# Differential attention mixer of a two-layer encoder: shorter vector work, some weight splitting on GpSimd, another order of steps

## The chip, the cores and the metric

The kernel runs on one core of a Trainium2 chip. The metric is the device time of one execution in microseconds, as the median of three runs. The engines are called PE (matmuls, with PEld for its weight loads), DVE (vector), ACT (scalar), POOL or GpSimd, and SP (which only issues DMAs here).

## What is computed

A trunk of two layers over 256 tokens of width 1024. Each layer is a half-step SwiGLU block (inner width 2816), a token mixer and a second half-step SwiGLU block, each behind an RMS norm. Layer 0 mixes with gated linear attention (GLA), layer 1 with differential attention, which the change is about:

```python
def diff_mixer(h, w_in, qk_norm_g, lam_vecs, subln_g, w_out, rel_table, lam_init):
    q, k, v = jnp.split(h @ w_in, [DIFF_QK, 2 * DIFF_QK], axis=-1)
    q = rms_norm(q.reshape(B, S, DIFF_HEADS, 2, DIFF_DH), qk_norm_g[0]) * (DIFF_DH ** -0.5)
    k = rms_norm(k.reshape(B, S, DIFF_HEADS, 2, DIFF_DH), qk_norm_g[1])
    ...
        p1 = jax.nn.softmax(jnp.einsum('bhqd,bhkd->bhqk', q1b, k1) + bias, axis=-1)
        p2 = jax.nn.softmax(jnp.einsum('bhqd,bhkd->bhqk', q2b, k2) + bias, axis=-1)
        return jnp.einsum('bhqk,bhkv->bhqv', p1 - lam * p2, vh)
    ...
    out = rms_norm(out, subln_g) * (1.0 - lam_init)
    return out.reshape(B, S, DIFF_V) @ w_out
```

There are 8 heads of 2 x 64 channels for q and k and 128 for v. All is float32.

## The kernel before

**Weights.** PE multiplies in a reduced form of float32 (`FR`), so each weight and each activation is held as a high part and a low part and each product is three matmuls. `weight_plan` (L61) lists all weight pieces in the order of use, numbered w0, w1 and so on. `prefetch` issues their DMAs on SP into three stage buffers; `parts` (L156) splits a staged piece in two halves of 128 x 1024 elements: ACT writes the high part (a copy, L192 in the profile, since both are issued from one helper line), DVE the low part, whole minus high (also L192). The results lie in five buffers `w`. A stage buffer is free again when its last low part is written. v's weights are pieces 125 and 126 (heads 0 to 3, in two halves of the inner dimension), 129 (heads 4 and 5) and 130 (heads 6 and 7); 131 to 134 belong to the output projection.

**The mixer** (`diff`, from L848). PE works on the projection in small pieces: a piece is 12 matmuls of 512 columns for q, k and the first v group, or 24 of 256 columns for the others. Heads go in four pairs. The steps of pair n are

- `b` qk_stats: from the sums of squares (L882 on ACT, L883 on DVE) the inverse square root of q's and k's mean squares, `dr`, and the scaled q and k, `qkx` (L900);
- `n` qk_norm: PE transposes them (L908), ACT and DVE write the high and low part (`qkn`);
- `s` softmax of one head: scores (L925), DVE adds the bias and takes the row maximum (L932), negates the maxima (L936), ACT takes the exponential and its sums (L940), DVE scales and subtracts the second map (L942 to L948);
- `f` flip: PE transposes the maps (L959);
- `a` attend: maps times v (L993), ACT squares (`dosq`, L997), DVE sums and takes the inverse root, `dro`, and writes the scaled output `do` (L1002);
- `o` normalize: PE transposes `do` (L1010), ACT and DVE write its parts for the output projection.

**The order.** The string `ORDER` (L46) lists these steps and pieces (`h`) as the program issues them. PE follows that order to the letter; the other engines run the instructions that the steps give them in an order that a scheduler fixes when the program is built. Every engine runs its own list strictly in sequence. `hold` keeps back weight splitting until the last pair is through. The last flip, attend and normalize stand inside the output projection. An inverse square root is the function `rsqrt` (L259): two integer steps for a first guess, then three Newton rounds of three instructions, 11 in all on DVE. It serves the norms, q and k (`dr`), the attention output (`dro`) and the GLA output.

Of the kernel before, what the change touches and what calls it, by code (L numbers as in the profile page):

```python
# [11 lines left out]
F32 = mybir.dt.float32  # L12
# [31 lines left out]


ORDER = """  # L46
h h h h h h b0 h h h n0 b1 h s00 s01 h n1 h h h f0 h s10 s11 h b2 h n2 a0 h f1 s20 s21 h a1 o0 h b3 h h f2 n3 o1 a2 s30 s31 h h o2 hold
"""


# [9 lines left out]

def weight_plan(w):  # L61

    plan = []

    def cols(a, start, width=CW, times=1, shift=BESIDE_X):
        plan.append((a[:, start : start + width], KD, width, times, shift))

    def wide(a, c, nk=KD, shift=WIDE_X):

        for k0 in range(0, nk, WK):  # L70
            n = min(WK, nk - k0)
            plan.append((a[k0 * P : (k0 + n) * P, c * WW : (c + 1) * WW], n, WW, 1, shift))

    def both(a, b):

        for k0 in range(0, KD, WK):
            plan.append((tuple(z[k0 * P : (k0 + WK) * P, :CW] for z in (a, b)), WK, WW, 1, WIDE_X))

    def ffn(i, j):
        gu, down = w["ffn_w_gu"][i, j], w["ffn_w_down"][i, j]  # L80
        for c in range(FF // CW):
            cols(gu, c * CW)
            cols(gu, FF + c * CW)
        if (i, j) == (1, 1):
            for c in range(D // WW):
                wide(down, c, NFB, WIDE_A)
            return
        for dc in range(D // CW):
            for k0 in range(0, NFB, KD):
                n = min(KD, NFB - k0)  # L90
                plan.append((down[k0 * P : (k0 + n) * P, dc * CW : (dc + 1) * CW], n, CW, 1, BESIDE_A))
# [12 lines left out]
    ffn(0, 1)  # L104
    ffn(1, 0)
    for kind, c in DIFF_COLS.split():
        a, c = w["diff_w_in"][0], int(c)
        if kind == "a":
            both(a[:, c * CW :], a[:, D + c * CW :])
        elif kind == "b":  # L110
            wide(a[:, 2 * D :], c)
        else:
            cols(a, 2 * D + c * CW)
    for c in range(4):
        cols(w["diff_w_out"][0], c * CW, shift=BESIDE_A)
    ffn(1, 1)
    return plan
# [3 lines left out]
def trunk(ctx: ExitStack, tc: tile.TileContext, ins, out):  # L121
# [34 lines left out]
    def parts():  # L156

        i = state["split"]
        _, nk, width, times, shift = plan[i]
        t = staged.pop(i)  # L160
        n = nk * 2 * times * width
        whole = wpool.tile([P, 2 * KD * CW + W_PAD], FR, tag="w", name=f"w{i}")
        w = split[i] = whole[:, shift : shift + n].rearrange("p (k h c) -> p k h c", h=2, c=times * width)
        state["split"] += 1
        step = 2 if i < 2 or width == WW else 4
        for k0 in range(0, nk, step):
            ks = slice(k0, min(k0 + step, nk))
            whole, wh, wl = t[:, ks, :], w[:, ks, 0, :], w[:, ks, 1, :]
            if times > 1:
                shape = [P, whole.shape[1], times, width]  # L170
                whole = whole[:, :, None, :].broadcast_to(shape)
                wh, wl = (z.rearrange("p k (c n) -> p k c n", c=times) for z in (wh, wl))
            high = partial(nc.scalar.activation, wh, whole, AF.Copy)
            low = partial(nc.vector.tensor_tensor, out=wl, in0=whole, in1=wh.bitcast(F32), op=ALU.subtract)
            yield high, low

    def split_weights(n):
# [93 lines left out]

# [576 lines left out]
    def diff(norm, nxt):  # L848
        with ExitStack() as octx:
# [21 lines left out]
            raw, tot, qkx, qkn, bias, sc, v_tm, dT, ov, eps = ({} for _ in range(10))  # L871

            def qk_done(hp):
                def done(t, pq):
                    raw[hp, t] = pq
                    if t == 0:
                        tot[hp] = small.tile([P, 2, 2, 4], F32, tag="dtot", name=f"dtot{hp}")
# [5 lines left out]
                    nc.vector.tensor_reduce(out=tot[hp][:, :, t], in_=sq.rearrange("p (i g d) -> p i g d", i=2, d=64), axis=AX.X, op=ALU.add)  # L883

                return done

            def qk_stats(hp):
# [3 lines left out]
                    src = bass.AP(frel_d.tensor, frel_d.offset + 2 * hp * (2 * T - 1) + P * qt, [[1, P], [2 * T - 1, 2], [1, T]])  # L891
                    nc.sync.dma_start(bias[hp][:, qt], src)

                for t in range(2):
                    nc.vector.tensor_scalar(out=tot[hp][:, :, t, :], in0=tot[hp][:, :, t, :], scalar1=1.0 / 64, scalar2=evx[:, t : t + 1], op0=ALU.mult, op1=ALU.add)
                r = rsqrt(tot[hp].rearrange("p i t g -> p (i t g)"), [P, 16], "dr").rearrange("p (i t g) -> p i t g", i=2, t=2)
                qkx[hp] = d2.tile([P, 2, 2, CW], F32, tag="qkx", name=f"qkx{hp}", bufs=1)
                for t in range(2):
                    v4 = [z.rearrange("p i (g d) -> p i g d", d=64) for z in (qkx[hp][:, :, t], raw.pop((hp, t)).rearrange("p (i c) -> p i c", i=2))]
                    nc.vector.tensor_tensor(out=v4[0], in0=v4[1], in1=r[:, :, t, :, None].broadcast_to([P, 2, 4, 64]), op=ALU.mult)  # L900
# [17 lines left out]
            def softmax(hp, b):  # L918
# [67 lines left out]
            def attend(c):  # L986
# [11 lines left out]
                nc.vector.scalar_tensor_tensor(out=dtot, in0=dtot, scalar=1.0 / P, in1=eps.pop(c), op0=ALU.mult, op1=ALU.add)  # L998
# [94 lines left out]
```

## Time and profile before

| | |
|---|---|
| runs shown | 994.36, 995.04, 996.09 us; median 995.04 |
| profiled execution | 995.94 us, its span in the profile 994.1 |
| busy | PE 983.7, DVE 745.6, ACT 565.3, POOL 1.4 us |
| PE's clock | full in every slice of the span |
| differential mixer | 686.2 to 803.0 us of the span |

The span is what the profile covers of the execution; 1.8 us lie around it. A line such as "PE a L1 <- DVE b L2: 1.8, 2, 0.9" says that PE, before the instruction of line 1 that writes a, waited in two places for DVE's instruction of line 2, 1.8 us in all. Matmuls are pipelined and their ends are modelled.

### The profile page before, as it was taken

Reading aid. Unit: us, or ns where it says so; the run is one execution under the profiler, and the core shown is the slowest. Engines: PE = TensorE matmul, PEld = TensorE weight load, DVE = VectorE, ACT = ScalarE, POOL = GpSimd, SP = SyncE. Lnnn points to the kernel's source line nnn. Section 1 sums busy time; section 2 is a strip of 40 time slices with the busy share of each in tenths; the row PEclk is TensorE's granted clock in tenths of the full one; section 3 lists DMA queues with packets and bytes.
Section 4 is the critical chain, followed back from the end, with each engine's and each line's share of the span. In section 5 each row is a group of like instructions: output and inputs, shape, how many; then the busy total and the mean of one; then the engine's idle time right before and its main releaser. Section 6 shows DMA issues by size and latency. Waiting matters only on the chain.

```text
span 994.1 us, 14886 instructions
## 1 busy us (share of the span) xinstructions
PE 983.7 (99%) x5890; PEld 871.5 (88%) x5890; DVE 745.6 (75%) x1275; ACT 565.3 (57%) x946; POOL 1.4 (0%) x9
## 2 busy tenths in 40 slices
PE   9999999999999999999999999999999999999998
PEld 8788888998889888888888888888788998888887
DVE  6988757499977997875679787556998699877640
ACT  6756545298756765643456555435486567665430
POOL 0000000000000000000000000000000000000000
PEclk9999999999999999999999999999999999999999
DMA  9776554665322775555557555475661258755530
GB/s 307 249 241 197 170 180 123 192 220 183 123 85 85 254 253 178 193 164 185 171 176 247 194 187 174 134 230 174 228 191 66 82 183 260 236 170 177 184 127 22
DMA packets 166787, 178.87 MB, mean 180 GB/s; under 512 B 4579, under 2 KB 155550, under 8 KB 166718
## 3 DMA queue, kind: packets, MB, share of 16 engines
q1 hardware_dynamic: 166318, 177.71, 55.3%
q8 instruction: 46, 0.75, 0.3%
q10 hardware_dynamic: 400, 0.21, 0.1%
q14 instruction: 23, 0.19, 0.1%
HBM read 176.84 MB, written 1.06 MB: 179 GB/s over the span
## 4 chain that ended last, share of the span: by engine, by line
PE 69%; DVE 4%; ACT 2%; issue 1%; DMA 0%; SPq 0%; ACTq 0%
PE ps_u L216 12%; PE ps_g L216 12%; PE ps_d L216 8%; PE ps_g L217 6%; PE ps_u L217 6%; PE ps_d L217 4%; PE ps_d L232 2%; PE ps_d L231 2%; PE ps_d L233 2%; DVE w L192 2%; PE ps_s L681 1%; PE ps_w L209 1%; PE ps_w L210 1%; PE ps_w L211 1%; PE ps_g L231 1%; PE ps_g L233 1%
## 5 line engine op out<-in xcount | busy, mean ns | idle before, releaser
L192 DVE TENSOR_TENSOR w<-stage,w 128x1024 fp32r<-128x1024 f32 x332 | 384.2, 1196 | 32.9 <-ACT w L192 32.7
L192 ACT ACTIVATE w<-stage 128x1024 fp32r<-128x1024 f32 x332 | 326.9, 1036 | 61.6 <-DMA stage<-in_ffn_w_gu_dram 16.1
L216 PE MATMUL ps_g<-x,w 128*128 128x512 f32 x704 | 246.6, 392 | 0.8 <-ACT w L506 0.8
L216 PE MATMUL ps_u<-x,w 128*128 128x512 f32 x704 | 246.3, 392 | 0.0
L217 PE MATMUL ps_u<-x,w 128*128 128x256 f32 x704 | 196.9, 280 | 0.0
L217 PE MATMUL ps_g<-x,w 128*128 128x256 f32 x704 | 196.5, 280 | 0.0
L216 PE MATMUL ps_d<-a,w 128*128 128x512 f32 x528 | 183.2, 390 | 0.0
L216 PEld LDWEIGHTS ps_g<-x,w 128*128 128x128 f32 x704 | 132.0, 188 | 30.5 <-ACT w L506 1.1
L216 PEld LDWEIGHTS ps_u<-x,w 128*128 128x128 f32 x704 | 132.2, 188 | 29.0
L217 PE MATMUL ps_d<-a,w 128*128 128x256 f32 x528 | 148.9, 282 | 0.0
L217 PEld LDWEIGHTS ps_g<-x,w 128*128 128x128 f32 x704 | 132.0, 188 | 0.3
L217 PEld LDWEIGHTS ps_u<-x,w 128*128 128x128 f32 x704 | 132.2, 188 | 0.0
L216 PEld LDWEIGHTS ps_d<-a,w 128*128 128x128 f32 x528 | 99.1, 188 | 20.8
L217 PEld LDWEIGHTS ps_d<-a,w 128*128 128x128 f32 x528 | 99.8, 189 | 0.0
L327 ACT ACTIVATE x<-x,par 128x256 fp32r<-128x256 f32 x40 | 20.0, 507 | 117.3 <-DVE x L380 117.3
L256 ACT COPY half<-ps_u 128x256 f32<-128x256 f32 x88 | 32.5, 370 | 81.8 <-PE ps_u L217 80.9
L256 ACT COPY half<-ps_g 128x256 f32<-128x256 f32 x88 | 32.1, 368 | 73.1 <-PE ps_g L217 72.2
L257 DVE TENSOR_TENSOR gate<-ps_g,half 128x256 f32<-128x256 f32 x88 | 36.6, 420 | 38.6 <-ACT half L256 38.6
L257 DVE TENSOR_TENSOR up<-ps_u,half 128x256 f32<-128x256 f32 x88 | 36.6, 420 | 36.4 <-ACT half L256 36.4
L380 DVE SCALAR_TENSOR_TENSOR x<-ps_d,x 128x256 f32<-128x256 f32 x48 | 20.3, 423 | 57.9 <-PE ps_d L217 56.6
L232 PE MATMUL ps_d<-w,a 128*128 128x512 f32 (+1 forms) x110 | 38.2, 347 | 0.0
L231 PE MATMUL ps_d<-w,a 128*128 128x512 f32 (+1 forms) x110 | 38.2, 347 | 0.0
(241 smaller groups left out, 1344.2 us busy)
## 6 DMA issues: line engine op xcount, KB each, us to landing
stage<-in_ffn_w_gu_dram SPq DMA_DIRECT2D x86, 1024.0 KB, 5.2
stage<-in_ffn_w_down_dram SPq DMA_DIRECT2D x34, 1024.0 KB, 5.3
stage<-in_gla_w_in_dram SPq DMA_DIRECT2D x12, 1024.0 KB, 6.7
stage<-in_ffn_w_down_dram SPq DMA_DIRECT2D x12, 768.0 KB, 4.4
stage<-in_diff_w_in_dram SPq DMA_DIRECT2D x16, 512.0 KB, 5.0
stage<-in_gla_w_out_dram SPq DMA_DIRECT2D x4, 1024.0 KB, 5.5
stage<-in_diff_w_in_dram SPq DMA_DIRECT2D x4, 1024.0 KB
stage<-in_diff_w_out_dram SPq DMA_DIRECT2D x4, 1024.0 KB, 5.7
```

What stands on the lines that cost most here:

```text
L192: op()
L209: mm(ps, lhsT=w[:, k, 0, ms], rhs=act[:, k, 0, :], start=first, stop=False)
L210: mm(ps, lhsT=w[:, k, 0, ms], rhs=act[:, k, 1, :], start=False, stop=False)
L216: mm(ps, lhsT=w[:, wk, 0, ms], rhs=act[:, k, :, :], start=first, stop=False)
L217: mm(ps[:, 0:T], lhsT=w[:, wk, 1, ms], rhs=act[:, k, 0, :], start=False, stop=last)
L231: mm(ps, lhsT=act[:, k, 0, ts_], rhs=w[:, wk, 0, cs], start=k == 0, stop=False)
L232: mm(ps, lhsT=act[:, k, 0, ts_], rhs=w[:, wk, 1, cs], start=False, stop=False)
L233: mm(ps, lhsT=act[:, k, 1, ts_], rhs=w[:, wk, 0, cs], start=False, stop=k == nk - 1)
L256: nc.scalar.copy(h[:, b, :], ps[:, T:512])
L257: nc.vector.tensor_tensor(out=out_t[:, b, :], in0=ps[:, 0:T], in1=h[:, b, :], op=ALU.add)
L327: high = nc.scalar.activation(self.x2[:, d, 0, :], src, AF.Copy, scale=g)
L380: nc.vector.scalar_tensor_tensor(out=x[:, d, :], in0=ps[:, h * T : (h + 1) * T], scalar=coef, in1=x[:, d, :], op0=ALU.mult, op1=ALU.add,)
```

## The change

Five edits:

- `rsqrt` has nine instructions: after the first guess one round of four and one of three.
- The affine step of the q/k statistics and the eps term of the output norm take one instruction for what was two (L895 and L946), with another layout of the sums.
- The scores are negated as the bias is added, so that the row minimum can go to the exponential as it is; the negation L936 is gone, and an exponential reads only its own minimum.
- The low parts of v's weights are written by GpSimd. Ahead of the first stands a library instruction.
- `ORDER` is another one.

In the changed file L192 is L193, and the lines of the mixer have numbers that are five to eight higher.

```diff
 ORDER = """
-h h h h h h b0 h h h n0 b1 h s00 s01 h n1 h h h f0 h s10 s11 h b2 h n2 a0 h f1 s20 s21 h a1 o0 h b3 h h f2 n3 o1 a2 s30 s31 h h o2 hold
+h h h h h b0 h h h n0 b1 h h s00 s01 n1 h h b2 h f0 h s10 s11 n2 h h h f1 h s20 s21 h a0 h b3 o0 a1 h n3 f2 o1 h s30 s31 a2 h h o2 hold
 """
...
-            wide(a[:, 2 * D :], c)
+            wide(a[:, 2 * D :], c, aside=True)
         else:
-            cols(a, 2 * D + c * CW)
+            cols(a, 2 * D + c * CW, aside=True)
...
-            low = partial(nc.vector.tensor_tensor, out=wl, in0=whole, in1=wh.bitcast(F32), op=ALU.subtract)
+            low = partial((nc.gpsimd if aside else nc.vector).tensor_tensor, out=wl, in0=whole, in1=wh.bitcast(F32), op=ALU.subtract)
...
-        for _ in range(3):
-            nc.vector.scalar_tensor_tensor(out=t, in0=y, scalar=-0.5, in1=y, op0=ALU.mult, op1=ALU.mult)
-            nc.vector.tensor_tensor(out=t, in0=t, in1=v, op=ALU.mult)
-            last = nc.vector.scalar_tensor_tensor(out=y, in0=t, scalar=1.5, in1=y, op0=ALU.add, op1=ALU.mult)
+
+        nc.vector.tensor_tensor(out=t, in0=y, in1=v, op=ALU.mult)
+        nc.vector.tensor_tensor(out=t, in0=t, in1=y, op=ALU.mult)
+        nc.vector.scalar_tensor_tensor(out=t, in0=t, scalar=-10.0 / 3.0, in1=t, op0=ALU.add, op1=ALU.mult)
+        nc.vector.scalar_tensor_tensor(out=y, in0=t, scalar=5.0, in1=y, op0=ALU.add, op1=ALU.mult)
+
+        nc.vector.scalar_tensor_tensor(out=t, in0=y, scalar=-0.5 * 0.375**3, in1=y, op0=ALU.mult, op1=ALU.mult)
+        nc.vector.tensor_tensor(out=t, in0=t, in1=v, op=ALU.mult)
+        last = nc.vector.scalar_tensor_tensor(out=y, in0=t, scalar=1.5 * 0.375, in1=y, op0=ALU.add, op1=ALU.mult)
...
-                for t in range(2):
-                    nc.vector.tensor_scalar(out=tot[hp][:, :, t, :], in0=tot[hp][:, :, t, :], scalar1=1.0 / 64, scalar2=evx[:, t : t + 1], op0=ALU.mult, op1=ALU.add)
...
+                nc.vector.scalar_tensor_tensor(out=tot[hp], in0=tot[hp], scalar=1.0 / 64, in1=evx[:, :, None].broadcast_to([P, 2, 8]), op0=ALU.mult, op1=ALU.add)
...
-                            out=s[c][:, qt, :], in0=ps[c][:, qt * T : (qt + 1) * T], in1=bias[hp][:, qt, b, :], scale=1.0,
-                            scalar=-3.0e38, op0=ALU.add, op1=ALU.max, accum_out=mx[:, 2 * c + qt : 2 * c + qt + 1],
+                            out=s[c][:, qt, :], in0=ps[c][:, qt * T : (qt + 1) * T], in1=bias[hp][:, qt, b, :], scale=-1.0,
+                            scalar=3.0e38, op0=ALU.add, op1=ALU.min, accum_out=mx[:, 2 * c + qt : 2 * c + qt + 1],
                         )
-                nc.vector.tensor_scalar(out=mx, in0=mx, scalar1=-1.0, scalar2=None, op0=ALU.mult)
...
-                        nc.scalar.activation(s[c][:, qt, :], s[c][:, qt, :], AF.Exp, bias=mx[:, j : j + 1], accum_out=sm[:, j : j + 1])
+                        nc.scalar.activation(s[c][:, qt, :], s[c][:, qt, :], AF.Exp, scale=-1.0, bias=mx[:, j : j + 1], accum_out=sm[:, j : j + 1])
```

On DVE, before the scaled q and k of pair 0 (`qkx`, here `qkx_6576`), the order was this. `w_6516` is piece 124, `w_6537` piece 125, `w_6610` piece 126 (weights of v); `dtot` are the sums of squares.

```order
L883 TENSOR_REDUCE dtot_6463<-dsq 128x2x4
L192 TENSOR_TENSOR w_6516<-stage_6423,w_6516 128x2x512
L192 TENSOR_TENSOR w_6537<-stage_6444,w_6537 128x2x512 x2
L883 TENSOR_REDUCE dtot_6554<-dsq 128x2x4
L895 TENSOR_SCALAR dtot_6463<-dtot_6463,evx 128x2x4
L895 TENSOR_SCALAR dtot_6554<-dtot_6554,evx 128x2x4
L263 TENSOR_SCALAR dr_t<-dtot_6463 128x16
L264 TENSOR_SCALAR dr_y<-dr_t 128x16
L266 SCALAR_TENSOR_TENSOR dr_t<-dr_y 128x16
...
L192 TENSOR_TENSOR w_6610<-stage_6514,w_6610 128x2x512
L900 TENSOR_TENSOR qkx_6576<-ps_da_0_6431,dr_y 128x2x256
```

It is now this, and GpSimd has the list under it, in which the four rows of weights are pieces 125, 126, 129 and 130:

```order
L889 TENSOR_REDUCE dtot_6451<-dsq 128x8
L193 TENSOR_TENSOR w_6502<-stage_6411,w_6502 128x2x512
L900 SCALAR_TENSOR_TENSOR dtot_6451<-dtot_6451,evx 128x16
L264 TENSOR_SCALAR dr_t<-dtot_6451 128x16
L265 TENSOR_SCALAR dr_y<-dr_t 128x16
L267 TENSOR_TENSOR dr_t<-dr_y,dtot_6451 128x16
L268 TENSOR_TENSOR dr_t<-dr_t,dr_y 128x16
...
L274 SCALAR_TENSOR_TENSOR dr_y<-dr_t,dr_y 128x16
L905 TENSOR_TENSOR qkx_6535<-ps_da_0_6419,dr_y 128x2x256
```

```order
L193 ISA
L193 TENSOR_TENSOR w_6541<-stage_6432,w_6541 128x2x512 x2
L193 TENSOR_TENSOR w_6626<-stage_6500,w_6626 128x2x512 x2
L193 TENSOR_TENSOR w_6824<-stage_6644,w_6824 128x4x256 x2
L193 TENSOR_TENSOR w_6947<-stage_6789,w_6947 128x4x256 x2
```

The low parts of pieces 125 and 126 are gone from between the sums and `qkx`, the root of pair 0 no longer waits for the sums of pair 1, and it is two steps shorter.

On ACT, the squares of the first output (`dosq` from `ps_do_6996`) stood right behind a high part of a weight, ahead of the exponentials of heads 4 and 5:

```order
L192 ACTIVATE w_7032<-stage_6815 128x4x256
L997 ACTIVATE dosq,dotot<-ps_do_6996 128x128 x4
L882 ACTIVATE dsq<-ps_da_0_6968 128x512
L960 COPY dT_7053<-ps_T_7054 128x512
L960 COPY dT_7053<-ps_T_7060 128x512
L940 ACTIVATE s_0_7080,sm<-s_0_7080,mx 128x256 x2
L940 ACTIVATE s_1_7081,sm<-s_1_7081,mx 128x256 x2
L940 ACTIVATE s_0_7113,sm<-s_0_7113,mx 128x256 x2
L940 ACTIVATE s_1_7114,sm<-s_1_7114,mx 128x256 x2
L997 ACTIVATE dosq,dotot<-ps_do_7144 128x128
```

Now those exponentials and both high parts of piece 132 (`w_7181`) stand ahead of the squares of the first output (from `ps_do_7075`):

```order
L968 COPY dT_6965<-ps_T_6972 128x512
L888 ACTIVATE dsq<-ps_da_0_6952 128x512
L947 ACTIVATE s_0_7015,sm<-s_0_7015,mx 128x256 x2
L947 ACTIVATE s_1_7016,sm<-s_1_7016,mx 128x256 x2
L947 ACTIVATE s_0_7045,sm<-s_0_7045,mx 128x256 x2
L947 ACTIVATE s_1_7046,sm<-s_1_7046,mx 128x256 x2
L193 ACTIVATE w_7181<-stage_6945 128x4x256 x2
L1005 ACTIVATE dosq,dotot<-ps_do_7075 128x128 x4
```

The squares moved from ahead of eight exponentials to behind them and behind two high parts. On PE the order is that of the string: between attend 0 and normalize 0 stood a piece, a flip, two heads' scores, a piece and attend 1; now there is one piece and, as the scheduler set it, seven of the eight products of attend 1.

## Rows read from the trace of the kernel before

**Rows 1.** Page, its first part: busy time, share of the span, instructions.

```profile
PE 983.7 (99%) x5890; PEld 871.5 (88%) x5890; DVE 745.6 (75%) x1275; ACT 565.3 (57%) x946; POOL 1.4 (0%) x9
```

**Rows 2.** Waits of PE: line, releaser, us in total, times, longest.

```profile
PE ps_sc L925 <- DVE qkx L900: 1.8, 2, 0.9
PE ps_r L357 <- DVE r_y L268: 1.3, 1, 1.3
PE ps_da L231 <- DVE do L1002: 1.1, 1, 1.1
...
PE ps_doT L1010 <- DVE do L1002: 0.7, 1, 0.7
PE ps_f L908 <- ACT dT L960: 0.2, 1, 0.2
PE ps_s L681 <- DVE qkd L721: 0.2, 1, 0.2
```

**Rows 3.** Busy time of each engine, the differential mixer's stretch.

```profile
686.20:803.00 116.80, 112.99 (x759) 100.28 (x758) 100.09 (x313) 75.17 (x178) 0.00 (x0) 1.00 0.49 155
```

**Rows 4.** DVE by line, that stretch: busy, mean ns, idle before.

```profile
L192 DVE TENSOR_TENSOR w<-stage,w 128x1024 fp32r<-128x1024 f32 x30 | 35.6, 1219 | 0.2 <-ACT w L192 0.2
L932 DVE CUSTOM_DVE_ANT_0 s<-ps_sc,bias 128x256 f32<-128x256 f32 x32 | 12.0, 420 | 0.0
...
L936 DVE TENSOR_SCALAR mx<-mx 128x4 f32<-128x4 f32 x8 | 1.3, 165 | 0.0
```

**Rows 5.** ACT by line and shape, the same stretch.

```profile
L192 ACT ACTIVATE w<-stage 128x1024 fp32r<-128x1024 f32 x30 | 30.1, 1052 | 11.9 <-PE ps_da L233 7.6 <-DMA stage<-in_diff_w_in_dram 2.4 <-PE ps_db L233 1.8
```

**Rows 6.** Timeline of DVE, second norm: start, us, instruction.

```profile
203.53 0.16 DVE L268 SCALAR_TENSOR_TENSOR r_y<-r_t,r_y 128x2 f32<-128x2 f32 x1
203.79 2.73 DVE L658 SCALAR_TENSOR_TENSOR z<-ps_z,r_y,bias 128x512 f32<-128x512 f32 x4
```

**Rows 7.** Timeline of ACT: high part, squares of output 0, exps.

```profile
744.57 1.04 ACT L192 ACTIVATE w<-stage 128x1024 fp32r<-128x1024 f32 x1
745.54 0.28 ACT L997 ACTIVATE dosq<-ps_do 128x128 f32<-128x128 f32 x1
...
745.94 0.28 ACT L997 ACTIVATE dosq<-ps_do 128x128 f32<-128x128 f32 x1
...
754.66 0.51 ACT L940 ACTIVATE s<-s,mx 128x256 f32<-128x256 f32 x1 [4.81 <-DVE mx L936]
...
755.17 0.49 ACT L940 ACTIVATE s<-s,mx 128x256 f32<-128x256 f32 x1
```

**Rows 8.** Timeline of DVE: root of output 0, low part, product.

```profile
747.34 0.17 DVE L263 TENSOR_SCALAR dro_t<-dotot 128x4 int32<-128x4 int32 x1
747.54 0.17 DVE L264 TENSOR_SCALAR dro_y<-dro_t 128x4 int32<-128x4 int32 x1
...
749.87 1.22 DVE L192 TENSOR_TENSOR w<-stage,w 128x1024 fp32r<-128x1024 f32 x1
751.01 0.69 DVE L1002 TENSOR_TENSOR do<-ps_do,dro_y 128x512 f32<-128x512 f32 x1
```

**Rows 9.** PE: scores, two matmuls (timeline), attend 1 (chain).

```profile
749.06 1.71 PE L925 MATMUL ps_sc<-qkn 64*128 64x256 f32 x24
...
752.38 0.39 PE L233 MATMUL ps_da<-w,x 128*128 128x512 f32 x1
752.61 0.39 PE L231 MATMUL ps_da<-w,x 128*128 128x512 f32 x1
...
754.81 1.78 PE ps_do L993 x16
```

**Rows 10.** Timeline of PE, two matmuls of v.

```profile
764.32 0.28 PE L231 MATMUL ps_dv<-w,x 128*128 128x256 f32 x1
764.44 0.29 PE L232 MATMUL ps_dv<-w,x 128*128 128x256 f32 x1
```

**Rows 11.** GpSimd by line and shape, whole span.

```profile
L306 POOL MEMSET w2t<- 128x1024 f32 x1 | 1.0, 955 | 50.4 <-ACT a L583 50.4
```

More of the change, by code (lines that the diff above doesn't have):

```diff
@@ L63, in weight_plan, with cols, wide @@
     plan = []
-    def cols(a, start, width=CW, times=1, shift=BESIDE_X):
-        plan.append((a[:, start : start + width], KD, width, times, shift))
-    def wide(a, c, nk=KD, shift=WIDE_X):
+    def cols(a, start, width=CW, times=1, shift=BESIDE_X, aside=False):
+        plan.append((a[:, start : start + width], KD, width, times, shift, aside))
+    def wide(a, c, nk=KD, shift=WIDE_X, aside=False):
         for k0 in range(0, nk, WK):
             n = min(WK, nk - k0)
-            plan.append((a[k0 * P : (k0 + n) * P, c * WW : (c + 1) * WW], n, WW, 1, shift))
+            plan.append((a[k0 * P : (k0 + n) * P, c * WW : (c + 1) * WW], n, WW, 1, shift, aside))
     def both(a, b):
         for k0 in range(0, KD, WK):
-            plan.append((tuple(z[k0 * P : (k0 + WK) * P, :CW] for z in (a, b)), WK, WW, 1, WIDE_X))
+            plan.append((tuple(z[k0 * P : (k0 + WK) * P, :CW] for z in (a, b)), WK, WW, 1, WIDE_X, False))
     def ffn(i, j):
@@ L90, in ffn @@
                 n = min(KD, NFB - k0)
-                plan.append((down[k0 * P : (k0 + n) * P, dc * CW : (dc + 1) * CW], n, CW, 1, BESIDE_A))
+                plan.append((down[k0 * P : (k0 + n) * P, dc * CW : (dc + 1) * CW], n, CW, 1, BESIDE_A, False))
     ffn(0, 0)
@@ L158, in parts @@
         i = state["split"]
-        _, nk, width, times, shift = plan[i]
+        _, nk, width, times, shift, aside = plan[i]
         t = staged.pop(i)
@@ L870, in diff @@
             d2 = octx.enter_context(tc.tile_pool(name="dif2", bufs=2))
-            raw, tot, qkx, qkn, bias, sc, v_tm, dT, ov, eps = ({} for _ in range(10))
+            raw, tot, qkx, qkn, bias, sc, v_tm, dT, ov, eps, sums = ({} for _ in range(11))
             def qk_done(hp):
@@ L876, in done @@
                     if t == 0:
-                        tot[hp] = small.tile([P, 2, 2, 4], F32, tag="dtot", name=f"dtot{hp}")
+                        tot[hp] = small.tile([P, 2, 8], F32, tag="dtot", name=f"dtot{hp}")
                         if hp == 0:
@@ L882, in done @@
                     nc.scalar.activation(sq, pq, AF.Square)
-                    nc.vector.tensor_reduce(out=tot[hp][:, :, t], in_=sq.rearrange("p (i g d) -> p i g d", i=2, d=64), axis=AX.X, op=ALU.add)
+                    nc.vector.tensor_reduce(out=tot[hp][:, t], in_=sq.rearrange("p (g d) -> p g d", d=64), axis=AX.X, op=ALU.add)
                 return done
@@ L892, in qk_stats @@
                     nc.sync.dma_start(bias[hp][:, qt], src)
-                for t in range(2):
-                    nc.vector.tensor_scalar(out=tot[hp][:, :, t, :], in0=tot[hp][:, :, t, :], scalar1=1.0 / 64, scalar2=evx[:, t : t + 1], op0=ALU.mult, op1=ALU.add)
-                r = rsqrt(tot[hp].rearrange("p i t g -> p (i t g)"), [P, 16], "dr").rearrange("p (i t g) -> p i t g", i=2, t=2)
+                nc.vector.scalar_tensor_tensor(out=tot[hp], in0=tot[hp], scalar=1.0 / 64, in1=evx[:, :, None].broadcast_to([P, 2, 8]), op0=ALU.mult, op1=ALU.add)
+                r = rsqrt(tot[hp].rearrange("p t g -> p (t g)"), [P, 16], "dr").rearrange("p (t i g) -> p t i g", i=2, t=2)
                 qkx[hp] = d2.tile([P, 2, 2, CW], F32, tag="qkx", name=f"qkx{hp}", bufs=1)
@@ L899, in qk_stats @@
                     v4 = [z.rearrange("p i (g d) -> p i g d", d=64) for z in (qkx[hp][:, :, t], raw.pop((hp, t)).rearrange("p (i c) -> p i c", i=2))]
-                    nc.vector.tensor_tensor(out=v4[0], in0=v4[1], in1=r[:, :, t, :, None].broadcast_to([P, 2, 4, 64]), op=ALU.mult)
+                    nc.vector.tensor_tensor(out=v4[0], in0=v4[1], in1=r[:, t, :, :, None].broadcast_to([P, 2, 4, 64]), op=ALU.mult)
             def qk_norm(hp):
@@ L928, in softmax @@
                 mx = small.tile([P, 4], F32, tag="mx", name="mx")
-                sm = small.tile([P, 4], F32, tag="sm", name="sm")
+                if b == 0:
+                    sums[hp] = small.tile([P, 2, 4], F32, tag="sm", name="sm")
+                sm = sums[hp][:, b]
                 for c in range(2):
@@ L939, in softmax @@
                         j = 2 * c + qt
-                        nc.scalar.activation(s[c][:, qt, :], s[c][:, qt, :], AF.Exp, bias=mx[:, j : j + 1], accum_out=sm[:, j : j + 1])
+                        nc.scalar.activation(s[c][:, qt, :], s[c][:, qt, :], AF.Exp, scale=-1.0, bias=mx[:, j : j + 1], accum_out=sm[:, j : j + 1])
                 nc.vector.reciprocal(out=sm[:, 2:4], in_=sm[:, 2:4])
                 nc.vector.scalar_tensor_tensor(out=sm[:, 2:4], in0=sm[:, 0:2], scalar=nlam, in1=sm[:, 2:4], op0=ALU.mult, op1=ALU.mult)
-                if b == 0:
-                    eps[hp] = small.tile([P, 4], F32, tag="deps", name=f"deps{hp}")
-                nc.vector.scalar_tensor_tensor(out=eps[hp][:, 2 * b : 2 * b + 2], in0=sm[:, 0:2], scalar=EPS, in1=sm[:, 0:2], op0=ALU.mult, op1=ALU.mult)
                 for qt in range(2):
                     nc.vector.scalar_tensor_tensor(out=s[0][:, qt, :], in0=s[1][:, qt, :], scalar=sm[:, 2 + qt : 3 + qt], in1=s[0][:, qt, :], op0=ALU.mult, op1=ALU.add)
+                if b == 1:
+                    eps[hp] = small.tile([P, 2, 2], F32, tag="deps", name=f"deps{hp}")
+                    first = sums.pop(hp)[:, :, 0:2]
+                    nc.vector.scalar_tensor_tensor(out=eps[hp], in0=first, scalar=EPS, in1=first, op0=ALU.mult, op1=ALU.mult)
             def flip(hp):
@@ L997, in attend @@
                         squared = nc.scalar.activation(sq, po[:, b, qt, :], AF.Square, accum_out=dtot[:, 2 * b + qt : 2 * b + qt + 1])
-                nc.vector.scalar_tensor_tensor(out=dtot, in0=dtot, scalar=1.0 / P, in1=eps.pop(c), op0=ALU.mult, op1=ALU.add)
+                nc.vector.scalar_tensor_tensor(out=dtot, in0=dtot, scalar=1.0 / P, in1=eps.pop(c).rearrange("p b q -> p (b q)"), op0=ALU.mult, op1=ALU.add)
                 ro = rsqrt(dtot, [P, 4], "dro")
```

## Prediction

> **What bounds the kernel now.** I read the page's shares first: PE is busy for 99% of the span [rows 1]. Then the chain of waits of PE over the whole span [rows 2]: outside the start-up it stops in seven places, five of them (four lines) in the differential mixer. Third, the stretch of that mixer, 686.2 to 803.0 us [rows 3]: PE 112.99 of 116.80 us, DVE 100.09, ACT 75.17, GpSimd nothing, PE's clock granted in full. So less work on DVE is worth only what it takes from PE's stops: 1.8 (twice, scores of a second head waiting for the scaled q and k, L900), 1.1 (a projection piece that waits for a PSUM bank which the product L1002 still reads), 0.7 (transposing that product) and 0.2, in all 3.8 us. A stop begins in these rows at the modelled end of the matmul before, 0.39 us after its start, while the next could start after 0.23 [rows 9]; some 0.16 more per stop and five stops make about 4.6 us. That is the most the mixer can give.
>
> **How the sum is made.** I laid the old and the new order out side by side: each instruction starts when its engine is free and what it reads is done, with the durations below. For the old order this gives stops of 1.2, 1.0, 0.7, 0.7 and 0.9, together 4.5 us, near the rows; so what I give for the new order is set against 4.5, and a single stop can be off by 0.5.
>
> **DVE's small edits.** Eight negations of the row maxima at 0.165 [rows 4] go, 1.3 us; merged steps of q/k statistics and of the eps terms save about 1.5; each of the eight inverse square roots in the mixer is two steps shorter at 0.20 from start to start [rows 8], 3.2; eight low parts at 1.22 [rows 4] go to GpSimd, 9.8. Some 16 of 100 us leave DVE. Exps need only their own row minimum and start earlier, by up to three of the four reductions of 0.42 [rows 4].
>
> **The two first stops go.** The scaled q/k of the second pair is walked to be done 0.7 us before the scores ask for it (old order: 1.2 late), that of the third 0.9 before. The stop at the bank goes too, since another piece of projection stands there.
>
> **A new stop at the first transposed output.** Old order: attend 0, then two pairs of scores, pieces and flips, then normalize 0. New: attend 0, one piece, most of attend 1, normalize 0. PE: scores of heads 4 and 5 started at 749.06 [rows 9]; now 1.78 earlier, as attend 0 [rows 9] is no longer ahead of them, and 2.1 for the two stops, so at about 745.1. Then 2.26 for the scores, a piece of 12 matmuls at 0.228 (2.73), 16 passes of attend 0 (1.78), another piece 2.73, 7/8 of attend 1 (1.56): PE stands at the transposition at 756.0. ACT: DVE is free for the first reduction at 746.7 (a sum of squares is ahead), exps begin at 747.1 and follow each other every 0.49 [rows 7]: eight end at 751.1. Now the two high parts of weight 132 stand **before** the squares of attend 0: 0.97 apiece [rows 7], 753.0. Four squares every 0.40 [rows 7]: 754.5. DVE: sum and eps 0.3, nine steps 1.7, product 0.69 [rows 8]: 757.2, PE starts at 757.35. Stop: 1.35 us. The same delay reaches the next two: q/k 3 is scaled behind this product, 0.35, and the flip that needs its PSUM bank, 0.25.
>
> **Third and last normalization.** For pair 2 ACT's last exp ends at 772.9, squares to 774.5, sum 0.2, nine steps 1.7: 776.4, then a low part of weight 133 stands ahead of the product, as one did in the old order [rows 8] (1.13), product 0.69: 778.15, PE 778.3. PE arrives after 48 matmuls of v at 0.12 [rows 10] and six of the output projection at 777.2. Stop 1.1; in the old order almost none. Pair 3, at the end: the chain is 0.4 shorter, but its transposition stands three matmuls (0.35) earlier: 0.9 stays. Sum: 1.35 + 0.35 + 0.25 + 1.1 + 0.9 = 3.95 against 4.5, **a gain of 0.5**.
>
> **Elsewhere.** The nine-step root also stands in every norm. At 203.53 its last step ends right before the gate sums [rows 6] that lead to the GLA scores' 0.2 us stop [rows 2]; between 0 and 0.4 earlier, I take 0.2. At 27.5 us PE waits 1.3 for a norm's root [rows 2]; the chain is 0.4 shorter and PE gets there two matmuls (0.35) earlier: nothing.
>
> **GpSimd's low parts.** The trace has no GpSimd instruction that reads SBUF. Bounds: below, its write of as many elements, 0.96 us [rows 11]; above, three such passes for two reads and a write, 2.87. For PE either end costs nothing: the high parts are there at 702.2, 707.2, 726.2 and 737.9, PE asks for the weights from 723, 726, 755 and 766, and with 2.87 apiece the closest pair is done 10 us early; the stage buffers they hold longer delay no load that PE sees up to some 5 us apiece. That also covers the added library instruction, which waits for nothing, and the moved bias loads, whose buffers come free earlier than before. The Trainium skill, "GPSIMD Engine Reference", § 3.1, has 4497 ns for such an addition of 2048 elements, so by estimate 2.25 us here; by that the sum above stays as it is. Its 2293 ns for VectorE agrees with the 1.22 for 1024 [rows 4].
>
> **Forecast.** -0.5 - 0.2 = -0.7 us. Against the profiled execution, 995.94, that is 995.2; that execution is 0.90 over the median of the three runs, 995.04, against which it is **994.3 us**. With the walk's errors this case holds 992.7 to 995.9. About 0.2%, 2.0 us, is what a measurement can tell from no change, so most of this case is "same".
>
> **Rival 1, slower: GpSimd's low part and DVE's root exclude each other.** If a DVE instruction with two SBUF inputs cannot run beside a GpSimd one that reads SBUF, low parts of weights 125 and 126 block the root of q/k 0, which the old order ran with GpSimd idle (seven of its nine steps read two SBUF operands). At 1.91 us apiece (two passes of [rows 11]) they hold 702.3 to 706.2 and 707.2 to 711.0; five steps fit into the gap, the rest end with the product at 712.1, and PE asked at 708.4: 3.8, and 0.5 for the second half. Those of weight 129 hold the root of q/k 2 the same way, 2.2 at the scores of head 3. That is 6.5 - 0.7 = +5.8: 1000.8 us. At 2.87 it is +12, 1007; under 1.8 apiece the steps fit into the gap and it costs at most 2. For it: all eight stand in a stretch where DVE's roots have 1 to 3 us of slack. Against it: nothing but the rows of ACT, whose high parts read the same stage tiles beside DVE's low parts at 1.05 us [rows 5], and ACT is another engine. This is the rule of the Trainium skill, "SBUF — State Buffer", § Who interferes with whom: the two share a port pair, taken for a whole instruction, and the other blocks. No run here shows it. By that rule with 2.25 us apiece the time would be about 1002. Chance 0.33; the rows bear out neither side, so it is held under the forecast.
>
> **Rival 2, faster: the new chains are shorter than laid out**, and of the new stops only the last remains, because ACT's high parts slip in between exps or PE comes later: 3.1 less, 994.3 - 3.1 = 991.2. For it: ACT is idle for a third of the stretch [rows 3]. Against it: each engine keeps its written order, and the two high parts stand ahead of the squares. Chance 0.12.
>
> **Rival 3, GpSimd is so slow (over 5 us apiece) that a later weight is late**, some 1000: at 5.5 apiece the walk gives 3 us more. Chance 0.05. The forecast itself has 0.5; that the change does nothing to the time lies inside it.
>
> **Range and chances.** 992.2 to 1003.5 leaves out a tenth at each side: most of rival 2 below, rival 1 from about 2.4 us apiece above. Faster: rival 2 and a sixth of the forecast, 0.20. Slower: rivals 1 and 3, 0.38, and 0.01 for the forecast's upper edge, 0.39. The rest, 0.41, is the same.
>
> **What would show it.** Right: PE no longer waits for L905 at the scores, waits about 1.3 at the transposition of product 0 and 1.1 at that of product 2, with the two high parts of weight 132 between the last exp and the first square on ACT; DVE's roots keep 0.2 a step. Rival 1: steps of the first and third q/k root stretched or spaced by one GpSimd instruction, and PE waiting at the first transposition of q/k. Wrong altogether: a stop at a projection piece for a weight, or PE losing more than 1 us at a place not named here.

## The result, and the profile after

The change is slower. Run beside the kernel before, its median was 1005.88 us (1005.18 to 1006.56, four runs) against 995.57: a ratio of 1.0099, 95% interval 1.0088 to 1.0111, so 10.3 us more. (A ratio here and below is the one on record with its interval; the quotient of the two medians, here 1.0104, lies inside the interval each time.) The profiled execution took 1006.03 us, its span 1004.2. The forecast, 994.3, is far off, and the time lies above the range's upper end of 1003.5. It is rival 1 that came, and more than it.

Page of the changed kernel, first part, to be held against [rows 1]:

```profile
PE 986.2 (98%) x5890; PEld 873.0 (87%) x5890; DVE 748.5 (75%) x1219; ACT 566.6 (56%) x946; POOL 20.4 (2%) x17
```

DVE has 56 instructions fewer than before and is busier all the same: something makes instructions longer. GpSimd now works 19 us more. Waits of PE in the mixer (line, releaser, us in total, times, longest), to be held against [rows 2]:

```profile
PE ps_f L913 <- DVE qkx L905: 4.9, 1, 4.9
PE ps_doT L1018 <- DVE do L1010: 3.1, 3, 1.4
PE ps_sc L930 <- DVE qkx L905: 2.3, 1, 2.3
```

Two lines are new, the first transposition of q/k (4.9) and the scores of head 3 (2.3); both wait for a scaled q/k. What holds them is on DVE. Its timeline at the root of q/k 0 (start, us, instruction):

```profile
701.89 2.38 DVE L900 SCALAR_TENSOR_TENSOR dtot<-dtot,evx 128x16 f32<-128x16 f32 x1
704.31 2.31 DVE L264 TENSOR_SCALAR dr_t<-dtot 128x16 int32<-128x16 int32 x1
706.66 0.17 DVE L265 TENSOR_SCALAR dr_y<-dr_t 128x16 int32<-128x16 int32 x1
...
707.08 2.26 DVE L268 TENSOR_TENSOR dr_t<-dr_t,dr_y 128x16 f32<-128x16 f32 x1
709.37 2.26 DVE L269 SCALAR_TENSOR_TENSOR dr_t<-dr_t 128x16 f32<-128x16 f32 x1
...
712.50 1.29 DVE L905 TENSOR_TENSOR qkx<-ps_da,dr_y 128x512 f32<-128x512 f32 x2
```

Steps that last 0.17 elsewhere [rows 8] take 2.3. GpSimd's timeline has the low parts of pieces 125, 126, 129 and 130, 2.4 us each:

```profile
701.73 4.86 POOL L193 TENSOR_TENSOR w<-stage,w 128x1024 fp32r<-128x1024 f32 x2 [505.41 <-ACT w L193]
706.92 4.67 POOL L193 TENSOR_TENSOR w<-stage,w 128x1024 fp32r<-128x1024 f32 x2 [0.33 <-ACT w L193]
732.26 4.74 POOL L193 TENSOR_TENSOR w<-stage,w 128x1024 fp32r<-128x1024 f32 x2 [20.66 <-ACT w L193]
748.27 4.78 POOL L193 TENSOR_TENSOR w<-stage,w 128x1024 fp32r<-128x1024 f32 x2 [11.27 <-ACT w L193]
```

One stretched step stands beside each GpSimd instruction: four beside pieces 125 and 126, and two beside piece 129, in the root of q/k 2. The steps at 0.17 fall into the gap from 706.59 to 706.92 or behind the last one. Beside piece 130 DVE only had low parts to write, for which PE did not wait.

The two new stops are 7.2 us. The rest is PE's clock. Windows of the changed kernel (stretch, its length, busy time of PE, PEld, DVE, ACT, POOL, granted clock, DMA share, GB/s), the first to be held against [rows 3]:

```profile
686.20:813.50 127.30, 116.85 (x759) 102.89 (x758) 105.02 (x272) 76.83 (x177) 19.05 (x8) 0.96 0.45 142
708.00:713.00 5.00, 0.46 (x3) 0.04 (x1) 4.79 (x7) 0.00 (x0) 3.59 (x2) 0.76 0.65 213
713.00:717.00 4.00, 3.61 (x12) 3.05 (x13) 3.28 (x6) 2.44 (x4) 0.00 (x0) 0.50 0.77 253
717.00:718.00 1.00, 1.00 (x5) 0.74 (x5) 0.86 (x6) 1.00 (x2) 0.00 (x0) 0.77 0.00 0
740.00:745.00 5.00, 4.90 (x24) 4.25 (x25) 4.89 (x22) 2.85 (x11) 0.00 (x0) 0.66 0.73 227
```

Behind both stops PE runs at 0.50 of its clock, the level of 1.2 GHz, for 3 to 4 us; at the first it had fallen while PE still stood (0.76 over 708 to 713, where PE works only until 708.5). PE's timeline shows it in the matmuls' starts:

```profile
708.08 0.39 PE L234 MATMUL ps_da<-w,x 128*128 128x512 f32 x1
713.33 2.26 PE L913 MATMUL ps_f<-cst,qkx 128*128 128x128 f32 x8 [4.87 <-DVE qkx L905]
715.25 0.78 PE L232 MATMUL ps_da<-w,x 128*128 128x512 f32 x1
715.82 0.63 PE L233 MATMUL ps_da<-w,x 128*128 128x512 f32 x1
716.25 0.63 PE L234 MATMUL ps_da<-w,x 128*128 128x512 f32 x1
...
717.50 0.39 PE L234 MATMUL ps_da<-w,x 128*128 128x512 f32 x1
717.74 0.40 PE L232 MATMUL ps_da<-w,x 128*128 128x512 f32 x1
```

Matmuls of the same size start 0.43 apart instead of 0.23 [rows 9]. The mixer is 127.30 - 116.80 = 10.5 us longer: PE stands still for 10.45 instead of 3.81 (+6.6: the new 7.2 and 3.1 at the output transpositions, for the 3.8 of before) and is busy for 116.85 instead of 112.99 (+3.9) with the same 759 rows of matmuls. The second term follows from the clock: half of 3.67 us from 713.33 to 717, 0.23 in the next, and 0.34 of the 5 us from 740 make 3.8.

### The profile page after: what moved, and what is told of

Read it like the earlier page. It is cut to its first block, busy times and chain, and to the rows that moved or that the text cites. A ratio compares the mean times of both kernels' runs of the same rounds, so it can differ in the third digit from the quotient of the medians.

```text
span 1004.2 us, 14855 instructions
## 1 busy us (share of the span) xinstructions
PE 986.2 (98%) x5890; PEld 873.0 (87%) x5890; DVE 748.5 (75%) x1219; ACT 566.6 (56%) x946; POOL 20.4 (2%) x17
## 4 chain that ended last, share of the span: by engine, by line
PE 91%; DVE 4%; ACT 2%; DMA 1%; issue 1%; SPq 0%; ACTq 0%
PE ps_u L217 16%; PE ps_g L217 15%; PE ps_d L217 12%; PE ps_u L218 8%; PE ps_g L218 8%; PE ps_d L218 6%; PE ps_d L233 2%; PE ps_d L232 2%; PE ps_d L234 2%; PE ps_s L687 2%; PE ps_w L210 1%; PE ps_w L211 1%; PE ps_w L212 1%; DMA stage<-in_ffn_w_gu_dram 1%; ACT s L947 1%
## 5 line engine op out<-in xcount | busy, mean ns | idle before, releaser
L193 DVE TENSOR_TENSOR w<-stage,w 128x1024 fp32r<-128x1024 f32 x324 | 376.8, 1201 | 34.3 <-ACT w L193 34.2
L193 ACT ACTIVATE w<-stage 128x1024 fp32r<-128x1024 f32 x332 | 326.8, 1036 | 48.7 <-PE ps_d L234 14.7
```

The lines of the kernel that those rows point to most:

```text
L193: op()
```

## Experiments

Theory 1: a GpSimd instruction that reads SBUF and a small DVE step on SBUF exclude each other, one step per instruction, and PE's clock falls behind the long stops. Rivals: the new order and the other edits cost the time; GpSimd is merely late, or any work of it disturbs.

### The change without GpSimd, and GpSimd alone

```diff
-            low = partial((nc.gpsimd if aside else nc.vector).tensor_tensor, out=wl, in0=whole, in1=wh.bitcast(F32), op=ALU.subtract)
+            low = partial(nc.vector.tensor_tensor, out=wl, in0=whole, in1=wh.bitcast(F32), op=ALU.subtract)
```

> The change, but with the low parts of v's weights on DVE again; all other edits stay. Theory 1 (GpSimd's low part, 2.4 us, and DVE's small steps on SBUF exclude each other, and PE's clock falls behind the long stops): the stops of 4.9 us at the first transposition of q/k and 2.3 us at the scores of head 3 go, the clock is granted in full in the mixer, the root steps keep 0.17 us; the stops at the output transpositions (1.35, 1.1, 0.9) and 0.35 at q/k 3 stay. The side-by-side layout gives 1.0 us less than before: 994 to 995.5. Rival (the new order and the other edits cost the 10 us): 1004 to 1006.

Measured: 995.39 us beside 994.93, ratio 0.9999 (0.9989 to 1.0008). Waits of PE in the mixer of this kernel:

```profile
PE ps_doT L1018 <- DVE do L1010: 3.1, 3, 1.4
PE ps_T L967 <- DVE s L952: 0.5, 1, 0.5
```

The two long stops are gone, the three at the output transpositions are as in the change, root steps take 0.17 again, and the clock is 1.00 throughout the mixer. Of the smaller stops expected, 0.35 at q/k 3 did not come, and 0.5 at a flip came unnamed. All of the loss hangs on GpSimd; order and other edits together neither cost nor gain.

The opposite: the kernel before, with this edit alone.

```diff
-            low = partial(nc.vector.tensor_tensor, out=wl, in0=whole, in1=wh.bitcast(F32), op=ALU.subtract)
+            low = partial((nc.gpsimd if 125 <= i <= 130 and i not in (127, 128) else nc.vector).tensor_tensor, out=wl, in0=whole, in1=wh.bitcast(F32), op=ALU.subtract)
```

> The kernel before with one edit: the low parts of v's weights (pieces 125, 126, 129, 130) on GpSimd; order, roots and negations as before. Theory 1: slower than before by 12 us from stops alone (4.2 + 0.5 at the first transposition of q/k, 1.8 at the first scores, 7.2 at the scores of head 3), and some 2 to 4 more where the clock falls: 1007 to 1012. Rival 1 (order and other edits cost): 994 to 996. Rival 2 (the split on GpSimd is only late, no exclusion): a stop at a projection piece of v for a weight, roots at 0.17 a step.

Measured: 1009.2 us, ratio 1.0133 (1.0118 to 1.0148), in theory 1's band. DVE's timeline in this kernel, at the root of q/k 0:

```profile
702.76 2.37 DVE L895 TENSOR_SCALAR dtot<-dtot,evx 128x8 f32<-128x8 f32 x1
705.16 2.32 DVE L263 TENSOR_SCALAR dr_t<-dtot 128x16 int32<-128x16 int32 x1
707.51 2.37 DVE L264 TENSOR_SCALAR dr_y<-dr_t 128x16 int32<-128x16 int32 x1
709.92 2.30 DVE L266 SCALAR_TENSOR_TENSOR dr_t<-dr_y 128x16 f32<-128x16 f32 x1
```

Its four GpSimd instructions run from 702.13 to 712.19, one step beside each, and PE waits 3.6 and, at the scores of head 3, 6.9 us; the 1.8 expected at the first scores did not come. The old order is no protection. Neither here nor in the change does PE wait in the mixer for a weight, so GpSimd is not merely late.

### What GpSimd must do to hold DVE off

GpSimd writes only:

```diff
+            if aside:
+                def low(z=wl.bitcast(F32)):
+                    for _ in range(3):
+                        nc.gpsimd.memset(z, 0.0)
```

> The change, where GpSimd only writes: in place of each low part it fills the same elements three times with zeros, some 2.9 us (3 x 0.96); the low parts of v's weights are left out. If only reads of SBUF by GpSimd exclude DVE: roots at 0.17 a step, no stop over 1.5 us in the mixer, 994 to 996. If any use of SBUF by GpSimd, or GpSimd's mere activity and the DMAs and weights around it, does it: root steps stretched to the length of a fill (0.96) or of three, stops of 3 us or more at the first transposition of q/k, 999 to 1008.

Measured: 996.89 us, ratio 1.0017 (1.0008 to 1.0026). DVE's timeline, while six of GpSimd's fills run from 696.29 to 701.71:

```profile
699.20 1.22 DVE L197 TENSOR_TENSOR w<-stage,w 128x1024 fp32r<-128x1024 f32 x1
700.33 0.17 DVE L904 SCALAR_TENSOR_TENSOR dtot<-dtot,evx 128x16 f32<-128x16 f32 x1
700.53 1.20 DVE L268 TENSOR_SCALAR dr_t<-dtot 128x16 int32<-128x16 int32 x1
701.77 0.17 DVE L269 TENSOR_SCALAR dr_y<-dr_t 128x16 int32<-128x16 int32 x1
```

Neither branch of the expectation holds whole; the time is 0.9 us above the first one's band. Instructions with two SBUF operands run beside fills at their normal 1.22 and 0.17. But a TENSOR_SCALAR stands until the last fill is through, here and at 724.58 for 2.57 us, and the second gives PE a stop of 1.4 at the scores of head 3.

GpSimd copies, one operand read:

```diff
+            if aside:
+                low = partial(nc.gpsimd.tensor_copy, out=wl, in_=whole)
```

> The change, where GpSimd copies the staged weight into the place of the low part (one operand read, one written) in place of the subtraction; the low parts of v's weights are wrong values then, the work around them is the same. If one read operand is enough to exclude DVE: root steps stretched to the copy's length; with a copy of 1.9 us 1000 to 1002, with one of 2.4 some 1005, under 1.3 at most 997. If it takes two read operands: 994 to 996 and roots at 0.17 a step, whatever the copy's length.

Measured: 994.25 us, ratio 0.9987 (0.9977 to 0.9997). DVE's timeline, beside copies from 702.49 to 705.52:

```profile
702.42 1.22 DVE L195 TENSOR_TENSOR w<-stage,w 128x1024 fp32r<-128x1024 f32 x1
703.55 1.01 DVE L902 SCALAR_TENSOR_TENSOR dtot<-dtot,evx 128x16 f32<-128x16 f32 x1
704.59 0.95 DVE L266 TENSOR_SCALAR dr_t<-dtot 128x16 int32<-128x16 int32 x1
```

One operand read is enough: two steps are stretched to a copy's 1.0. At that length they cost PE nothing (the branch "under 1.3"); the other copies met no root, so this run has fewer collisions than the change and not only shorter ones. The two copies took 3.03 and not 2.03 as the next pair did: the first waited for DVE's low part at 702.42, so the exclusion works both ways.

Each low part in four pieces:

```diff
+                    for k in range(z.shape[1]):
+                        for c in range(0, z.shape[2], 256):
+                            s = (slice(None), k, slice(c, c + 256))
+                            nc.gpsimd.tensor_tensor(out=z[s], in0=x[s], in1=h[s], op=ALU.subtract)
```

> The change, with each low part on GpSimd cut into four instructions of 128 x 256 elements (32 in place of 8; same reads, same writes). If a GpSimd instruction holds DVE off for its whole length and one DVE step slips in between two: steps of the roots stretched to the short length (about 0.6 to 0.8 by a quarter of 2.4), ten steps need some 7 us in place of 10.6, the stop at the first transposition falls from 4.9 to 1 to 3 and that at head 3 goes or falls under 2, so the clock stays up too: 996 to 1000. If the two only share the bandwidth, or a DVE step waits until GpSimd has nothing left: stops as in the change, 1003 to 1007.

Measured: 1001.73 us, ratio 1.0068 (1.0053 to 1.0083). DVE's timeline, with GpSimd's sixteen instructions from 700.22 to 711.41:

```profile
700.32 0.71 DVE L906 SCALAR_TENSOR_TENSOR dtot<-dtot,evx 128x16 f32<-128x16 f32 x1
...
706.63 0.65 DVE L280 SCALAR_TENSOR_TENSOR dr_y<-dr_t,dr_y 128x16 f32<-128x16 f32 x1
707.32 1.29 DVE L911 TENSOR_TENSOR qkx<-ps_da,dr_y 128x512 f32<-128x512 f32 x2
708.53 0.68 DVE L895 TENSOR_REDUCE dtot<-dsq 128x8 f32<-128x512 f32 x1
```

The mechanism is as expected: all ten steps take a short GpSimd instruction's 0.66, they need 7.0 us, and the first stop falls to 1.2. The product with an operand in PSUM (1.29 for two, as in the change behind GpSimd's last) and the sum over one SBUF tensor (0.68) pass beside GpSimd unstretched. The time is 1.7 us above the band: the stop at head 3 is 3.3, not under 2, and behind it the clock is 0.50 from 735 to 740.

### The two stops apart

GpSimd for pieces 129 and 130 only:

```diff
+            low = partial((nc.gpsimd if i in (129, 130) else nc.vector).tensor_tensor, out=wl, in0=whole, in1=wh.bitcast(F32), op=ALU.subtract)
```

> The change, with GpSimd writing the low parts of pieces 129 and 130 only; those of 125 and 126 are on DVE again. Theory 1 (exclusion, one small DVE step per GpSimd instruction of 2.4 us): no stop at the first transposition of q/k, root of q/k 0 at 0.17 a step; a stop of 2 to 4 us at the scores of head 3 as in the change, two steps of the root of q/k 2 stretched to 2.3, the clock lower for some us behind it: 997 to 1000. Rival (the 10 us come as a block, from GpSimd being used at all, its library load or one late piece): 1004 to 1006, or 994 to 996.

Measured: 1000.06 us, ratio 1.0053 (1.0036 to 1.0070). The time is at the upper end of the band; the profiled execution, 1002.47, is the slowest of the four. Nothing at the first transposition; 4.1 at the scores of head 3, a little over the 2 to 4 expected: PE comes there 6.8 us earlier than in the change, GpSimd's piece 129 only 4.6 (727.62 for 732.26). The stop among PE's waits in the mixer, and a window of PE's clock behind the stop:

```profile
PE ps_sc L930 <- DVE qkx L905: 4.1, 1, 4.1
```

```profile
735.00:740.00 5.00, 4.98 (x21) 4.44 (x22) 4.89 (x21) 2.93 (x12) 0.00 (x0) 0.50 0.77 258
```

So the loss is no block that comes with any use of GpSimd; each collision has its own price.

### PE kept at work in the stop

```diff
+                if hp == 0:
+                    busy = psB.tile([P, 512], F32, tag="B", name="ps_busy")
+                    for _ in range(22):
+                        mm(busy[:, 0:P], lhsT=warm.broadcast_to([P, P]), rhs=warm.broadcast_to([P, P]), start=True, stop=True)
```

> The change, with 22 matmuls of 128 columns into a bank that nobody reads, ahead of the first transposition of q/k: PE works through some 4.7 us (0.213 each, from the same kind at the start of the program) of the stop. The scheduler moves q/k 0's low parts behind the second root on DVE, which by the layout costs 1.7 at the scores of head 0 and gives 0.9 back at those of head 3. If the clock falls because PE stands still: the granted clock stays at 1.00 at 713 to 717, the matmuls behind the transpositions start 0.23 apart instead of 0.43, and the time is 0.8 - 2.1 = 1.3 under the change's: 1003.5 to 1005.5. If it falls for another reason (GpSimd's load, the transpositions themselves): 0.50 and 0.43 as before, 1006 to 1008.

Measured: 1004.63 us, ratio 1.0099 (1.0079 to 1.0119), three of four runs within 1004.12 to 1004.64, one at 1008.23. PE's timeline, and windows of its clock:

```profile
706.91 5.07 PE L912 MATMUL ps_busy<-warm 128*128 128x128 f32 x44
711.82 1.40 PE L917 MATMUL ps_f<-cst,qkx 128*128 128x128 f32 x8
...
713.52 0.39 PE L234 MATMUL ps_da<-w,x 128*128 128x512 f32 x1
713.75 0.39 PE L232 MATMUL ps_da<-w,x 128*128 128x512 f32 x1
```

```profile
708.00:718.00 10.00, 9.86 (x66) 8.79 (x65) 8.79 (x20) 3.56 (x5) 2.20 (x1) 1.00 0.50 156
722.00:725.00 3.00, 3.00 (x16) 2.68 (x14) 2.88 (x19) 2.94 (x12) 0.00 (x0) 0.50 0.38 130
740.00:745.00 5.00, 5.00 (x32) 4.28 (x33) 4.88 (x21) 3.03 (x13) 0.00 (x0) 1.00 0.68 224
```

Eight transpositions take 1.40 and not 2.26, matmuls start 0.23 apart, and the clock is 1.00 from 708 to 718, with GpSimd working as in the change. So at this stop the clock fell because PE stood still. But not every stop brings it down: in this run it fell to 0.50 (722 to 725) behind 1.6 us at the scores of head 0, a stop that the edit brings, and stayed at 1.00 (740 to 745) behind 2.0 at the scores of head 3, where 2.3 in the change was followed by 0.50. The time lies in the expected band, but its ratio is that of the change and its interval reaches over the 1.3 us at stake; the rows show the clock's part, the time doesn't.

### The order by itself

GpSimd with the order string of before:

```diff
-h h h h h b0 h h h n0 b1 h h s00 s01 n1 h h b2 h f0 h s10 s11 n2 h h h f1 h s20 s21 h a0 h b3 o0 a1 h n3 f2 o1 h s30 s31 a2 h h o2 hold
+h h h h h h b0 h h h n0 b1 h s00 s01 h n1 h h h f0 h s10 s11 h b2 h n2 a0 h f1 s20 s21 h a1 o0 h b3 h h f2 n3 o1 a2 s30 s31 h h o2 hold
```

> The change with the order string of before (GpSimd, nine-step roots, merged steps, negated scores stay). Theory 1, one DVE step per GpSimd instruction: the layout gives stops of 2.9 and 1.1 at the first transposition of q/k, 1.5 at the first scores, 1.3 at the scores of head 3, 3.5 us more than before, and 1 to 3 for the clock behind them: 999 to 1003, so 3 to 7 under the change. If the order has no part in it (exclusion costs the same in either): 1003 to 1006, less than 3 under the change.

Measured: 1004.38 us, ratio 1.0077 (1.0053 to 1.0101); four runs at 1004.3 to 1004.4, one at 999.12. It misses the band of theory 1's layout and lies in the other branch's, 1003 to 1006. Waits of PE in the mixer:

```profile
PE ps_sc L930 <- DVE qkx L905: 5.8, 1, 5.8
PE ps_f L913 <- DVE qkx L905: 2.8, 2, 2.0
```

Pieces 129 and 130 (730.78 to 736.44 and 737.59 to 742.23) both fall on the root of q/k 2 here, which the layout had not placed so; the first two and the last two of its ten steps are stretched. The exclusion is the same, its price depends on which steps each piece meets. The new order is not what makes the collisions.

The same, with all low parts on DVE as in the first run:

```diff
-            low = partial((nc.gpsimd if aside else nc.vector).tensor_tensor, out=wl, in0=whole, in1=wh.bitcast(F32), op=ALU.subtract)
+            low = partial(nc.vector.tensor_tensor, out=wl, in0=whole, in1=wh.bitcast(F32), op=ALU.subtract)
```

> The change without GpSimd and with the order string of before: what is left are the nine-step roots, the merged steps and the negated scores. Side by side the layout has stops of 0.8 (scores of head 0), 0.7 (transposition of q/k 3) and 0.9 (output 3) where before had 4.5, so 2.5 us less than before: 992 to 993.5. If those edits bring nothing on the path: 994 to 996. If the new order was what helped in the run without GpSimd: above that run's 995.4.

Measured: 992.88 us, ratio 0.9968 (0.9959 to 0.9977), 3 us under before. Waits of PE in the mixer, the three largest:

```profile
PE ps_doT L1018 <- DVE do L1010: 0.7, 1, 0.7
PE ps_da L232 <- DVE do L1010: 0.4, 1, 0.4
PE ps_sc L930 <- DVE qkn L921: 0.3, 1, 0.3
```

Nine-step roots, merged steps and negated scores together are worth these 3 us, and the new order alone gives them back at the output transpositions. Then with one token moved:

```diff
-h h h h h h b0 h h h n0 b1 h s00 s01 h n1 h h h f0 h s10 s11 h b2 h n2 a0 h f1 s20 s21 h a1 o0 h b3 h h f2 n3 o1 a2 s30 s31 h h o2 hold
+h h h h h h b0 h h n0 h b1 h s00 s01 h n1 h h h f0 h s10 s11 h b2 h n2 a0 h f1 s20 s21 h a1 o0 h b3 h h f2 n3 o1 a2 s30 s31 h h o2 hold
```

> As the run without GpSimd and with the order string of before, but the first transposition of q/k stands one piece earlier (the tokens h n0 swapped to n0 h), so that the low parts of q/k 0 stand ahead of the second root on DVE. The side-by-side layout takes the 0.8 us stop at the scores of head 0 away: 3.3 us less than before, 991 to 993. If the stop there isn't in that run, no difference to it.

Measured: 992.12 us, ratio 0.9963 (0.9948 to 0.9977). The 0.3 at the scores is gone from PE's waits; between this and the run above the intervals cannot tell. Both beat the kernel before and the change.

## Why the prediction was wrong

**The step that failed** is "GpSimd's low parts": "For PE either end costs nothing". I priced the instructions on GpSimd and asked only when their results are due, and gave the exclusion of DVE 0.33, because the trace of before has no GpSimd instruction that reads SBUF and "the rows bear out neither side". The run without GpSimd (0.9999) against the change (1.0099) shows that this step carries the whole error.

**Rival 1** had the mechanism, the two places and the sign: first and third root stretched, PE waiting at the first transposition and at head 3. Two sizes were off. An instruction is 2.40 us, not the 1.91 taken. At about 2.4 the prediction's range puts rival 1 at 1003.5, which is stops of some 9 us; they were 4.9 + 2.3 = 7.2, for one step got through with each GpSimd instruction, where rival 1 let steps through only in the gap. The Trainium skill, "GPSIMD Engine Reference", § 3.1, gave 2.25 by estimate; the measured 2.40 decides. And the clock was left out: 3.8 us by the windows. For the part behind the first stop, 2.1, the run with matmuls in it shows the cause; the part behind the second is read from the rows alone. Rival 1 also said that only steps with two SBUF operands are held; integer steps with one (L264) were held as well.

The Trainium skill, "SBUF — State Buffer", § Who interferes with whom, has the rule: two SBUF inputs collide with a GpSimd instruction that reads; `tensor_scalar`, where it runs in a mode that uses both ports, collides too; `tensor_reduce` never does; the lock lasts a whole instruction. The rows agree: 2.3 for 0.17 beside the subtraction, 1.0 beside the copy, 1.20 for the TENSOR_SCALAR alone beside fills, 0.68 for the sum. In which mode the TENSOR_SCALAR ran no trace shows.

**Most of the rest held.** The stops at the output transpositions were given as 1.35, 1.1 and 0.9. PE's timeline of the change:

```profile
767.67 0.63 PE L1018 MATMUL ps_doT<-cst,do 128*128 128x128 f32 x4 [1.43 <-DVE do L1010]
...
788.55 0.63 PE L1018 MATMUL ps_doT<-cst,do 128*128 128x128 f32 x4 [0.98 <-DVE do L1010]
...
799.87 0.63 PE L1018 MATMUL ps_doT<-cst,do 128*128 128x128 f32 x4 [0.67 <-DVE do L1010]
```

With the 0.16 that the modelled ends hide these are 1.6, 1.1 and 0.8. (The terms of the walk to the first add up to 756.16, not to the 756.0 written, which is well inside the 0.5 that it allows.) The two small stops behind them, 0.35 at q/k 3 and 0.25 at the flip after it, did not come: PE's waits have neither. On ACT both high parts of piece 132 (761.31, 1.99 us) stood ahead of the first square (763.20), as forecast. The bank's stop and those of the second heads' scores went, as the run without GpSimd shows. The forecast's -0.7 us, a ratio of 0.9993, lies inside that run's interval. So the other four edits together were costed rightly, at next to nothing. That three of them would have gained 3 us with the old order was not asked.

## What to carry to other kernels

Before work goes to GpSimd, look at what DVE does in the same microseconds: beside a GpSimd instruction that reads SBUF, every DVE step on two SBUF operands and every TENSOR_SCALAR of the roots waited for the whole of it, so a 0.17 us step on a critical chain became one of 2.3. Keep such chains apart from GpSimd's reads, or give GpSimd short instructions (which still cost 0.7% here), and price a PE stop with the slow clock that can stand behind it. Try the parts of a combined change alone: here three of five edits were worth 3 us, the order gave that back, and GpSimd lost 10.

## What the runs showed of the hardware that was not expected

- PE's clock: 0.50 (1.2 GHz) for some 4 us behind standing still 4.9 us in the change, and 0.50 for 5 us and more behind 4.1 us with GpSimd on pieces 129 and 130 only; full again after that. It stayed at 1.00 when PE multiplied through the same time. At the scores of head 3 it fell for 3 to 4 us behind stops of 1.4 (beside fills) and 2.3 us (the change), but not behind one of 2.0 (matmuls in the first stop); at the first output transposition it stayed at 1.00 behind 1.4 us in the change and 2.0 us in the run with matmuls. So the length of the stop alone does not decide. What does was not tried.
- Between GpSimd instructions that read, one DVE step slips in at each border. Between back-to-back fills of 0.96 us none did: a TENSOR_SCALAR waited 2.57 us, until the last of them had ended.
